# Two matmuls per weight block instead of three in a decoder trunk's input projection, with a weight ring of four buffers

## The chip, the cores and the metric

The kernel runs on one core of a Trainium2 chip. The metric is the device time of one execution in microseconds, the median over runs.

## What is computed

Two layers of a decoder trunk over 256 positions of width 2048. In each layer the input is normalised, projected to 5656 columns, split among three mixers (sparse attention, an S5 state space, causal mean pooling), gated by SiLU, and projected back:

```python
for l in range(DEPTH):
    h = rms_norm(x, norm_pre[l])
    proj = jnp.einsum('bsd,de->bse', h, w_in[l])
    (q, kc, vc, ksl, vsl, kwn, vwn, gl, z_att,
     u_s5, z_s5, u_pool, z_pool) = jnp.split(proj, split_points, axis=-1)
    att = nsa_mixer(...) * jax.nn.silu(z_att)
    ssm = s5_mixer(u_s5, ...) * jax.nn.silu(z_s5)
    pool = pool_mixer(u_pool, pool_w[l], pool_scale[l]) * jax.nn.silu(z_pool)
    mix = jnp.concatenate([att, ssm, pool], axis=-1)
    out = jnp.einsum('bse,ed->bsd', mix, w_out[l])
    x = x + rms_norm(out, norm_post[l])
```

The attention also compresses keys and values: blocks of 32 positions go through a weight of 32 x 128 x 256 (`cmp_w1_k`, `cmp_w1_v`) and a second of 256 x 128.

## The kernel before

All arithmetic is to float32's accuracy on float32r matmuls: each operand is split into a high and a low part, and a product takes three matmuls, high by high, high by low, low by high (`mm3`, lines 384 to 389). The normalised activations lie transposed in two tiles `hT` (new_hT, line 445), the high and the low part, each 128 partitions x 16 k tiles x 256 positions.

The weights come as a stream of pieces in a fixed order (`piece_plan`, line 35), each of two halves of 128 x 1024 floats. Per layer: `vs` 0 and 1, `u5` 0 to 3, then `kc` 0, `kc` 1, `vc` 0, `ck` 0, `ck` 1, `vc` 1, `ck` 2, `ck` 3, `ks` 0, `cv` 0, `cv` 1, `ks` 1, `cv` 2, `cv` 3, `kw` 0, `kw` 1, `vw` 0 to 2, then `q`, `za` and `z5`, `gl`, `up` and `zp`, and sixteen `wo` of the output projection. Forty of a layer's pieces (`u5`, `kc`, `vc`, `ks`, `kw`, `q`, `za`, `z5`, `up`, `zp`) go through `do_b` (line 893): 128 weight columns by all 256 positions, 16 blocks of `mm3` into the first 256 columns of one `pp` bank of PSUM (`mm_b`, line 885), then an evacuation `ev` that reads the bank: a ScalarE copy for `u5`, `q`, `up`; rotary embedding (`rope`, line 694, three VectorE operations on the bank) for `ks`, `kw`, `q`; `cmp_blocks` (line 636) for `kc`, `vc`; `silu2` for the gates. `vw` goes the other way round, and `ck` and `cv` multiply the raw float32 weights without a split (line 1111).

`load` (line 273) issues a half on SyncE's queue into a ring of `RAWB` = 5 `raw` buffers. `split` (line 291) makes the high part on ScalarE (line 311) and the low part on VectorE (line 317) into rings of four `whi` and four `wlo`; after that the raw buffer is free. A `ck` or `cv` half frees its buffer when TensorE has multiplied it. At the start of piece n the piece n + 3 is loaded, and during piece n the halves of n + 1 are split:

```python
    def do_b(n, evac):
        p = pp()
        for h in range(2):
            split(n + 1, h)
            mm_b(n, h, p)
            if h == 1:
                break
            slot(1.41)
        evac(p)
        slot(1.6)
```

Other work (the S5 chain, attention heads, pooling) is written as generators that `slot` advances between halves. The order in which each engine issues is then fixed by the framework's scheduler, which moves instructions by its own model of durations; only the start, and the border between the layers, keep the written order. At the border two stores of the layer's result (`xs`, line 1237) stand on SyncE's queue among the loads.

Of the kernel before, what the change touches and what calls it, by code (L numbers as in the profile page):

```python
# [29 lines left out]
# column offsets of the input projection  # L30
# [4 lines left out]
def piece_plan():  # L35
    """Weight pieces of one layer in the order of use: (kind, index, cols per half)."""
# [40 lines left out]
# columns of the per-layer small parameters  # L77
# [7 lines left out]
# columns of the per-layer S5 matrices, pool and compression matrices  # L85
# [52 lines left out]
def body(ctx, tc, a):  # L138
# [66 lines left out]
    def after(key):  # L205
        """issue what follows behind the instruction kept under key, on its engine"""
        return tc.issue_after(X[key].ins)

    def s5_params():
# [42 lines left out]
        # cos and sin of 4 theta b and 32 theta a, a and b in 0 .. 7  # L252
# [38 lines left out]
    def split(n, h, hold=False):  # L291
# [8 lines left out]
        if k == "wo" and i in (12, 13):  # L300
            if i == 12 and h == 0:
                X["hTw"] = tuple(z.rearrange("p k s -> p (k s)") for z in new_hT())
            o = ((i - 12) * 2 + h) * 1024
            hi, lo = (z[:, o:o + 1024] for z in X["hTw"])
        elif k == "vs" and 2 * i + h < 3:
            z = m8([128, 2048], F32R)
            hi, lo = z[:, :1024], z[:, 1024:]
        else:
            hi = wpool.tile([128, 1024], F32R, name=nm("whi"), tag="whi", bufs=4)
            lo = wpool.tile([128, 1024], F32R, name=nm("wlo"), tag="wlo", bufs=4)  # L310
# [29 lines left out]
    def grab(*tags):  # L340
        """wait until every one of the tags has a free buffer, then hold them"""
        while not all(free(g) for g in tags):
            yield 0.0
        for g in tags:
            take(g)

    def demand(*tags):
        """the same for the stream of pieces: run the chains until the buffers are free"""
        while not all(free(g) for g in tags):
            forced[0] += 1  # L350
            slot(2.0)
        for g in tags:
            take(g)
# [21 lines left out]
    def split_f32r(hi, lo, src, scale=None, hi_eng=None):  # L375
        """hi + lo == src * scale, both float32r"""
# [7 lines left out]
    def mm3(out, l, r, start, stop, **kw):  # L384
        """three passes: hi*hi, hi*lo, lo*hi"""
# [6 lines left out]
    def rstd_of(parts_, first=None):  # L392
        """(sum of the four parts / D + EPS) ** -0.5; first: what rstd_first made of three of them"""
# [11 lines left out]
    def norm_scale(x, r, gpre, hbuf, c):  # L405
        """hbuf = x * r * gpre in quarter c of x and hbuf [128, D]"""
# [3 lines left out]
    def norm_high(t, hbuf, hT, c):  # L410
        """high part of quarter c of hbuf transposed; returns what makes the low part"""
# [12 lines left out]
    def vsel(n, t, c):  # L424
        """values of the selected branch, tile t, from quarter c of hT"""
# [5 lines left out]
    def norm_vsel(n, t, x, r, gpre, hbuf, hT, lag):  # L431
        """the norm of tile t and its values, quarter after quarter"""
# [12 lines left out]
    def new_hT():  # L445
        return tuple(big.tile([128, NKT, S], F32R, name=nm("hT"), tag=f"hT{i}", bufs=1) for i in range(2))

# [1 line left out]
    def s5_chain(l):  # L449
# [22 lines left out]
        def tables(hf):  # L472
            """cos and sin of 4 theta j, j = 8 a + b, for the state tiles 8 hf .. 8 hf + 7"""
# [29 lines left out]
        def spread(dst, x, y, op, k0):  # L503
            """x op y, group by group into the block diagonal of dst"""
# [43 lines left out]
        for t in range(4):  # L548
# [5 lines left out]
            # transposed input matrices and the lag kernels  # L554
# [81 lines left out]
    def cmp_blocks(which, g, p, l):  # L636
# [3 lines left out]
        pv = p[:, :256].rearrange("p (n j) -> p j n", j=16)  # L640
# [53 lines left out]
    def rope(p, dst_hi, dst_lo):  # L694
        r1 = st([128, 256], "r1", bufs=2)
        r2 = st([128, 256], "r2", bufs=2)
        V.tensor_tensor(r1, p[:, :256], C["cos"], op=ALU.mult)
        V.tensor_tensor(r2[0:64], p[64:128, :256], C["sin"][64:128], op=ALU.mult)
        V.tensor_tensor(r2[64:128], p[0:64, :256], C["sin"][0:64], op=ALU.mult)
# [4 lines left out]
    def att_unit(pr, j, t):  # L704
        """one head of the pair, one tile of queries: scores .. transposed weights"""
# [173 lines left out]
    def silu2(dst, p):  # L879
        """dst = 2*silu(p)"""  # L880
# [4 lines left out]
    def mm_b(n, h, p):  # L885
        hi, lo = parts.pop((n, h))
        hT = X["hT"]
        for kk in range(8):
            k = 8 * h + kk
            sl = slice(kk * 128, kk * 128 + 128)  # L890
            mm3(p[:, :256], (hi[:, sl], lo[:, sl]), (hT[0][:, k, :], hT[1][:, k, :]), k == 0, k == 15)
# [40 lines left out]
    # start  # L932
# [91 lines left out]
    while n < nst:  # L1024
# [5 lines left out]
        if kind == "u5":  # L1030
# [12 lines left out]
            def ev(p, i=i):  # L1043
                A.activation(X["uT"][:, i, :], p[:, :256], AF.Copy)
                A.activation(X["utb"][:, i], p[:, :256].rearrange("p (j b) -> p b j", b=4), AF.Copy)
# [8 lines left out]
        elif kind in ("kc", "vc"):  # L1054
# [8 lines left out]
            def ev(p, i=i, w=w, l=l):  # L1063
                cmp_blocks(w, i, p, l)

            do_b(n, ev)
        elif kind in ("ks", "kw"):
# [3 lines left out]
            do_b(n, lambda p, i=i, b=b: rope(p, X["kr"][:, 0, i, b, :], X["kr"][:, 1, i, b, :]))  # L1071
# [44 lines left out]
        elif kind in ("q", "za"):  # L1116
# [9 lines left out]
            def ev(p, j=j, pr=pr, kind=kind):  # L1126
                if kind == "q":
                    A.activation(pr["qf"][:, j, :], p[:, :256], AF.Copy)
                    rope(p, pr["qr"][:, 0, j], pr["qr"][:, 1, j])
# [8 lines left out]
                else:  # L1138
                    silu2(pr["zt"][:, j, :], p[:, :256])
# [4 lines left out]
        elif kind == "z5":  # L1144
            if i == 0:
                X["z5"] = a8([128, 4, 256])
            do_b(n, lambda p, i=i: silu2(X["z5"][:, i, :], p[:, :256]))
# [28 lines left out]
        elif kind == "up":  # L1176
            def ev(p, i=i, l=l):
# [3 lines left out]
                A.activation(pu[:, 16:], p[:, :256], AF.Copy)  # L1181
# [3 lines left out]
        elif kind == "zp":  # L1185
            def ev(p, i=i):
                demand("zs")
                z = st([128, 2, 256], "zs", bufs=2)[:, 0]
                silu2(z, p[:, :256])
                X["zp", i] = z  # L1190
            do_b(n, ev)
        else:
# [32 lines left out]
            def update(t, r, sq=None):  # L1225
                """x += og * r, with the sums of squares or the store"""
# [80 lines left out]
RAWB = 5  # L1307
# [81 lines left out]
```

## Time and profile before

| | |
|---|---|
| median of 3 runs | 892.03 us (891.52 to 892.59) |
| span of the profiled execution, first to last instruction | 890.6 us |
| TensorE matmul busy | 857.6 us, 96% |
| TensorE weight load busy (beside matmuls) | 795.3 us, 89% |
| VectorE busy | 645.3 us, 72% |
| ScalarE busy | 481.3 us, 54% |
| GpSimd busy | 51.8 us, 6% |
| weight loads of 512 KB | 272, median 3.6 us from issue to landing |

The page gives no device time of the profiled execution beyond its span. Matmuls overlap in the trace: a busy time per matmul is longer than the step from one start to the next, and it is the step that counts. A row of the timeline gives the start, the time from the first start to the last end, engine, line, operation, tiles and the number of records merged.

### The profile page before, as it was taken

How to read it: one execution, taken by the hardware profiler on the slowest of the kernel's cores; microseconds unless marked ns; L12 is line 12 of the kernel's file. 1: busy time of each engine (PE TensorE's matmuls, PEld its weight loads, DVE VectorE, ACT ScalarE, POOL GpSimd, SP SyncE). 2: the span in 40 equal slices, each digit the busy share in tenths (PEclk: the TensorE clock that was granted, in tenths of full speed). 3: DMA queues.
4: the chain of work that ended last, by engine and by line, in shares of the span. 5: the costliest groups of instructions: out<-in, count | busy, mean ns of one | idle time of the engine just before them, and what ended most of it. 6: DMA issues, size and time to landing. Idle time of an engine off the chain costs nothing. (4 is left out here: it accounts for less than half of the span.)

```text
span 890.6 us, 17313 instructions
## 1 busy us (share of the span) xinstructions
PE 857.6 (96%) x6848; PEld 795.3 (89%) x6848; DVE 645.3 (72%) x1264; ACT 481.3 (54%) x933; POOL 51.8 (6%) x71
## 2 busy tenths in 40 slices
PE   4899999999999999999979999999999999999996
PEld 3898889999999999888869988999999999998884
DVE  6886779796987866556478556978968878665563
ACT  5454635676566754445445525475847767344440
POOL 3302000000000000000040300000000000000000
PEclk9899999999999999999989999999999999999998
DMA  7565766524344665456445558663534347455642
GB/s 288 179 188 185 268 235 225 172 104 162 121 165 143 227 241 194 172 201 224 182 165 199 183 197 312 211 213 99 173 123 155 140 144 295 154 177 189 197 146 95
DMA packets 46042, 165.75 MB, mean 186 GB/s; under 512 B 5508, under 2 KB 5764, under 8 KB 44808
## 3 DMA queue, kind: packets, MB, share of 16 engines
q1 hardware_dynamic: 43352, 154.15, 50.3%
q0 software_dynamic: 2608, 10.49, 3.3%
q8 instruction: 54, 0.88, 0.4%
q14 instruction: 28, 0.23, 0.1%
HBM read 159.37 MB, written 4.19 MB: 184 GB/s over the span
## 5 line engine op out<-in xcount | busy, mean ns | idle before, releaser
L311 ACT ACTIVATE whi<-raw 128x1024 fp32r<-128x1024 f32 (+2 forms) x238 | 248.4, 1046 | 256.3 <-PE pp L388 82.8
L317 DVE TENSOR_TENSOR wlo<-raw,whi 128x1024 fp32r<-128x1024 f32 (+1 forms) x236 | 284.4, 1207 | 123.7 <-ACT whi L311 123.1
L389 PE MATMUL pp<-hT,wlo 128*128 128x256 f32 x1280 | 365.7, 286 | 0.5 <-DVE wlo L317 0.5
L387 PE MATMUL pp<-hT,whi 128*128 128x256 f32 x1280 | 364.8, 285 | 0.8 <-ACT whi L311 0.8
L388 PE MATMUL pp<-hT,whi 128*128 128x256 f32 x1280 | 363.5, 284 | 0.0
L387 PEld LDWEIGHTS pp<-hT,whi 128*128 128x128 f32 x1280 | 245.0, 191 | 6.1 <-issue 3.8
L389 PEld LDWEIGHTS pp<-hT,wlo 128*128 128x128 f32 x1280 | 245.0, 191 | 2.4 <-DVE wlo L317 0.7
L388 PEld LDWEIGHTS pp<-hT,whi 128*128 128x128 f32 x1280 | 245.0, 191 | 1.7 <-issue 1.0
L387 PE MATMUL acc<-whi,m 128*128 128x512 f32 x112 | 44.4, 397 | 0.0
L389 PE MATMUL acc<-whi,m 128*128 128x512 f32 x112 | 44.4, 397 | 0.0
L388 PE MATMUL acc<-wlo,m 128*128 128x512 f32 x112 | 44.1, 394 | 0.0
L388 PE MATMUL pp<-wlo,m 128*128 128x512 f32 x112 | 43.6, 389 | 0.0
L389 PE MATMUL pp<-whi,m 128*128 128x512 f32 x112 | 43.6, 389 | 0.0
L387 PE MATMUL pp<-whi,m 128*128 128x512 f32 x112 | 43.6, 389 | 0.0
L507 ACT ACTIVATE m<-m 64x256 f32<-64x256 f32 x64 | 26.4, 413 | 5.9 <-DVE m L505 4.9
L728 ACT ACTIVATE P<-sc,sv 128x128 f32<-128x128 f32 (+1 forms) x64 | 26.2, 418 | 5.4 <-DVE sv L726 3.7
L925 POOL DMA_DIRECT2D a<-in_gpost x2 | 1.1, 557 | 451.4 <-PE tr L743 451.4
L378 ACT ACTIVATE a<-tr 128x256 fp32r<-128x256 f32 (+1 forms) x32 | 15.6, 488 | 18.6 <-PE tr L743 18.5
L387 PEld LDWEIGHTS acc<-whi,m 128*128 128x128 f32 x112 | 21.5, 192 | 4.5
L388 PEld LDWEIGHTS acc<-wlo,m 128*128 128x128 f32 x112 | 21.5, 192 | 4.5
L389 PEld LDWEIGHTS acc<-whi,m 128*128 128x128 f32 x112 | 21.4, 191 | 4.5
L736 ACT ACTIVATE P<-P,sv 128x128 f32<-128x128 f32 (+1 forms) x64 | 25.4, 448 | 0.0
(295 smaller groups left out, 1384.4 us busy)
## 6 DMA issues: line engine op xcount, KB each, us to landing
raw<-in_w SPq DMA_DIRECT2D x272, 512.0 KB, 3.6
raw<-in_w SPq DMA_DIRECT2D x8, 420.0 KB, 4.2
a<-in_x SPq DMA_DIRECT2D x4, 512.0 KB, 6.9
a<-in_gpost POOLq DMA_DIRECT2D x2, 1024.0 KB, 4.8
a<-in_x POOLq DMA_DIRECT2D x2, 1024.0 KB, 6.3
xs<-a SPq DMA_DIRECT2D x2, 1024.0 KB, 4.1
a<-xs POOLq DMA_DIRECT2D x2, 1024.0 KB, 7.4
out_dram<-a SPq DMA_DIRECT2D x8, 256.0 KB, 2.4
```

Source lines behind the costliest of these rows:

```text
L311: A.activation(hi[:, :w], raw[:, :w], AF.Copy)
L317: V.tensor_tensor(lo[:, :w], raw[:, :w], hi[:, :w].bitcast(F32), op=ALU.subtract)
L378: A.activation(hi, src, AF.Copy)
L387: T.matmul(out, lhsT=lh, rhs=rh, start=start, stop=False, **kw)
L388: T.matmul(out, lhsT=lh, rhs=rl, start=False, stop=False, **kw)
L389: T.matmul(out, lhsT=ll, rhs=rh, start=False, stop=stop, **kw)
L507: A.activation(dst[64 * g:64 * g + 64, :, k0:k0 + 4, 16 * g:16 * g + 16], x[64 * g:64 * g + 64], AF.Copy)
L728: A.activation(P[:, b], pv[:, b], AF.Exp, scale=SCALE, bias=sv[:, 1, b:b + 1], accum_out=sv[:, 2, b:b + 1])
L736: A.activation(P[:, b], P[:, b], AF.Copy, scale=sv[:, 4, b:b + 1])
L925: nc.gpsimd.dma_start(g, bass.AP(tensor=src.tensor, offset=src.offset, ap=[[0, 128], [1, D]]))
```

## The change

In `do_b` pieces a block takes two matmuls. Both activation halves lie in one tile, so the high weights multiply 512 columns at once, high activations into the first half of the bank and low activations into the second; the low weights then multiply the high activations into the first half. The two halves are added when the bank is emptied: `join` copies the second half to SBUF on ScalarE and adds it to the first on VectorE, and the evacuations read the sum from SBUF. For `u5`, `q` and `up` the join replaces the ScalarE copy. Two tiles `jn` and `jz` of two buffers each are new, and the ring of raw weights has four buffers instead of five.

```diff
-            mm3(p[:, :256], (hi[:, sl], lo[:, sl]), (hT[0][:, k, :], hT[1][:, k, :]), k == 0, k == 15)
+            mm2(p, (hi[:, sl], lo[:, sl]), hT[2][:, :, k, :], k == 0, k == 15)
...
+    def mm2(p, l, r, start, stop):
+        T.matmul(p.rearrange("p (z s) -> p z s", z=2), lhsT=l[0], rhs=r, start=start, stop=False)
+        T.matmul(p[:, :256], lhsT=l[1], rhs=r[:, 0], start=False, stop=stop)
+
+    def join(p, dst=None):
+        y = st([128, 256], "jn", bufs=2) if dst is None else dst
+        z = st([128, 256], "jz", bufs=2)
+        A.activation(z, p[:, 256:], AF.Copy)
+        V.tensor_tensor(y, p[:, :256], z, op=ALU.add)
+        return y
...
-        return tuple(big.tile([128, NKT, S], F32R, name=nm("hT"), tag=f"hT{i}", bufs=1) for i in range(2))
+        z = big.tile([128, 2, NKT, S], F32R, name=nm("hT"), tag="hT", bufs=1)
+        return z[:, 0], z[:, 1], z
...
-                A.activation(X["uT"][:, i, :], p[:, :256], AF.Copy)
-                A.activation(X["utb"][:, i], p[:, :256].rearrange("p (j b) -> p b j", b=4), AF.Copy)
+                u = join(p, X["uT"][:, i, :])
+                A.activation(X["utb"][:, i], u.rearrange("p (j b) -> p b j", b=4), AF.Copy)
...
-                cmp_blocks(w, i, p, l)
+                cmp_blocks(w, i, join(p), l)
...
-            do_b(n, lambda p, i=i, b=b: rope(p, X["kr"][:, 0, i, b, :], X["kr"][:, 1, i, b, :]))
+            do_b(n, lambda p, i=i, b=b: rope(join(p), X["kr"][:, 0, i, b, :], X["kr"][:, 1, i, b, :]))
...
-                    A.activation(pr["qf"][:, j, :], p[:, :256], AF.Copy)
-                    rope(p, pr["qr"][:, 0, j], pr["qr"][:, 1, j])
+                    rope(join(p, pr["qf"][:, j, :]), pr["qr"][:, 0, j], pr["qr"][:, 1, j])
...
-                    silu2(pr["zt"][:, j, :], p[:, :256])
+                    silu2(pr["zt"][:, j, :], join(p))
...
-                A.activation(pu[:, 16:], p[:, :256], AF.Copy)
+                join(p, pu[:, 16:])
...
-RAWB = 5
+RAWB = 4
```

The gates of `z5` and `zp` get the same `join`. The scheduler orders the new program anew, so instructions move on every engine.

SyncE's queue, first layer, the loads of `vc` 1, `ck` 2, `ck` 3 and `ks` 0, two halves each. In brackets is whom a load waits for to have its buffer: the load that filled it last (DMAHW), and the engine that read it last, DVE (VectorE) for a half that was split, PE (TensorE) for a `ck` or `cv` half. Before:

```order
L285 DMA raw_884<-in_w 128x1024 [waits DMAHW1_49,DVE_49]
L285 DMA raw_886<-in_w 128x1024 [waits DMAHW6_49,DVE_49]
L285 DMA raw_951<-in_w 128x1024 [waits DMAHW2_49,PE_49]
L285 DMA raw_953<-in_w 128x1024 [waits DMAHW3_49,PE_49]
L285 DMA raw_980<-in_w 128x1024 [waits DMAHW7_49,DVE_49]
L285 DMA raw_982<-in_w 128x1024 [waits DMAHW4_49,PE_49]
L285 DMA raw_1006<-in_w 128x1024 [waits DMAHW5_49,PE_49]
L285 DMA raw_1008<-in_w 128x1024 [waits DMAHW0_49,PE_49]
```

And in the changed kernel:

```order
L285 DMA raw_803<-in_w 128x1024 [waits DMAHW2_49,PE_49]
L285 DMA raw_805<-in_w 128x1024 [waits DMAHW3_49,PE_49]
L285 DMA raw_858<-in_w 128x1024 [waits DMAHW4_49,PE_49]
L285 DMA raw_860<-in_w 128x1024 [waits DMAHW5_49,PE_49]
L285 DMA raw_887<-in_w 128x1024 [waits DMAHW6_49,DVE_49]
L285 DMA raw_889<-in_w 128x1024 [waits DMAHW7_49,DVE_49]
L285 DMA raw_913<-in_w 128x1024 [waits DMAHW0_49,PE_49]
L285 DMA raw_915<-in_w 128x1024 [waits DMAHW1_49,PE_49]
```

The two loads of `vc` 1 waited for splits and now wait for TensorE's `ck` 0; those of `ks` 0 wait for TensorE in both, now for the two halves of `ck` 2.

TensorE's order in the changed kernel where `kw` 0 (bank pp_1277) goes from its first half to its second and `kw` 1 (pp_1342) begins; whi_1265 and wlo_1266 are `kw` 0's second half, whi_1278 is `kw` 1's first:

```order
L394 MATMUL pp_1277<-hT_84,wlo_1258 128x256
L668 MATMUL sc_1365<-cn,P_1336 128x32 x2
L393 MATMUL pp_1277<-hT_84,whi_1265 128x512
L393 MATMUL pp_1342<-hT_84,whi_1278 128x512
L394 MATMUL pp_1277<-hT_84,wlo_1266 128x256
```

Before, no matmul of `kw` 1 (pp_1483) stood in there; its first came behind the last of `kw` 0 (pp_1406):

```order
L388 MATMUL pp_1406<-hT_85,whi_1394 128x256
L389 MATMUL pp_1406<-hT_84,wlo_1395 128x256
L387 MATMUL pp_1483<-hT_84,whi_1407 128x256
```

A matmul of `kw` 1 has moved ahead of fifteen matmuls of `kw` 0.

VectorE's order around the low split of `ks` 0's first half, in the changed kernel (L610 and L611 are the S5 chain's products with the bank that the L601 matmuls fill, L656 is `cmp_blocks`, L401 the join's add):

```order
L610 TENSOR_TENSOR m_67_454<-sc_873,m_65_452 128x4x2x64
L611 TENSOR_TENSOR m_66_453<-sc_873,m_65_452 128x4x2x64
L401 TENSOR_TENSOR jn_952<-pp_917,jz_953 128x256
L614 TENSOR_TENSOR m_67_454<-m_67_454,m_66_453 128x256
L615 TENSOR_TENSOR m_67_454<-m_67_454,m_66_453 128x256
L656 TENSOR_TENSOR a_120_807<-jn_952,sm 128x16x15 x2
L317 TENSOR_TENSOR wlo_1015<-raw_913,whi_1014 128x1024
```

And before, where these products (L596 and following) stood one piece earlier and the operations ahead of the split are others of the S5 chain:

```order
L609 TENSOR_TENSOR m_68_463<-m_68_463,m_67_462 128x256
L610 TENSOR_TENSOR m_68_463<-m_68_463,m_67_462 128x256
L517 TENSOR_TENSOR m_68_463<-a_60_428,akt 128x256
L522 TENSOR_TENSOR m_67_462<-a_60_428,akt 128x256
L518 TENSOR_TENSOR m_68_463<-a_60_428,akt 128x256
L317 TENSOR_TENSOR wlo_1120<-raw_1006,whi_1119 128x1024
```

The products of that step of the S5 chain, and with them a wait for TensorE, have moved ahead of the low split.

## Rows read from the trace of the kernel before

**Rows 1.** The page, busy time by engine (us, share of the span, instructions).

```profile
PE 857.6 (96%) x6848; PEld 795.3 (89%) x6848; DVE 645.3 (72%) x1264; ACT 481.3 (54%) x933; POOL 51.8 (6%) x71
```

**Rows 2.** The page, the chain that ended last, shares of the span by line.

```profile
PE pp L387 11%; PE pp L388 11%; PE pp L389 11%; PE acc L388 2%; PE acc L389 2%; PE acc L387 2%; DMA raw<-in_w 1%; PE sc L587 1%; PE tr L743 1%; PE acc L592 1%; PE acc L1111 1%; ACT mr L930 0%; PE acc L615 0%; PE sc L389 0%; PE sc L387 0%
```

**Rows 3.** The page's groups: one of three lines (busy us, mean ns).

```profile
L389 PE MATMUL pp<-hT,wlo 128*128 128x256 f32 x1280 | 365.7, 286 | 0.5 <-DVE wlo L317 0.5
```

**Rows 4.** Timeline of TensorE, 500 to 504 us, first and last (start, length).

```profile
499.97 0.28 PE L387 MATMUL pp<-hT,whi 128*128 128x256 f32 x1
...
503.93 0.28 PE L387 MATMUL pp<-hT,whi 128*128 128x256 f32 x1
```

**Rows 5.** The chain that ended last in order of time (start, length).

```profile
522.01 6.44 DMA raw<-in_w
528.53 1.07 ACT whi L311
529.62 1.23 DVE wlo L317
```

**Rows 6.** Timeline of TensorE in the output projection, first and last.

```profile
377.90 0.39 PE L388 MATMUL pp<-wlo,m 128*128 128x512 f32 x1
...
385.83 0.39 PE L387 MATMUL pp<-whi,m 128*128 128x512 f32 x1
```

**Rows 7.** Timeline of TensorE, 615 to 616 us: three of 512 columns among 256s.

```profile
615.35 0.40 PE L387 MATMUL sc<-a,qr 128*128 128x512 f32 x1
...
616.05 0.28 PE L389 MATMUL pp<-hT,wlo 128*128 128x256 f32 x1
```

**Rows 8.** Groups by line: a VectorE operation and a ScalarE copy of a bank.

```profile
L697 DVE TENSOR_TENSOR r<-pp,cn 128x256 f32<-128x256 f32 x24 | 10.0, 416 | 8.6 <-PE pp L389 8.6
L1128 ACT ACTIVATE qf<-pp 128x256 f32<-128x256 f32 x16 | 5.9, 370 | 0.0
```

**Rows 9.** Windows (us; PE, PEld, DVE, ACT, POOL busy; PEclk, DMA share, GB/s).

```profile
120.00:140.00 20.00, 19.75 (x216) 19.40 (x217) 19.82 (x40) 9.63 (x18) 0.00 (x0) 1.00 0.66 225
...
160.00:180.00 20.00, 20.00 (x176) 18.56 (x175) 13.68 (x35) 11.28 (x29) 0.00 (x0) 1.00 0.44 154
180.00:200.00 20.00, 20.00 (x217) 19.44 (x217) 19.75 (x49) 14.81 (x37) 0.00 (x0) 1.00 0.30 107
```

**Rows 10.** Timeline, 93 to 102 us: from `ck` matmuls to `ks` 0's second half.

```profile
93.71 1.07 PE L1111 MATMUL acc<-raw,a 128*32 128x256 f32 x16
...
94.41 0.33 SPq L285 DMA_DIRECT2D raw<-in_w  x1
...
98.03 1.06 ACT L311 ACTIVATE whi<-raw 128x1024 fp32r<-128x1024 f32 x1 [1.49 <-DMA raw<-in_w]
...
99.12 1.23 DVE L317 TENSOR_TENSOR wlo<-raw,whi 128x1024 fp32r<-128x1024 f32 x1 [0.94 <-ACT whi L311]
...
101.73 0.36 PE L389 MATMUL pp<-hT,wlo 128*128 128x256 f32 x1
```

**Rows 11.** Timeline of SyncE's queue at the border of the layers.

```profile
462.20 0.33 SPq L1237 DMA_DIRECT2D xs<-a  x1
473.40 6.93 SPq L285 DMA_DIRECT2D raw<-in_w  x5
```

**Rows 12.** Timeline of TensorE, 105 to 109 us: `ck` and S5 matmuls.

```profile
105.80 1.05 PE L1111 MATMUL acc<-raw,a 128*32 128x256 f32 x16
106.78 0.66 PE L563 MATMUL tr<-cn,m 128*128 128x128 f32 x4
107.23 0.39 PE L387 MATMUL pp<-hT,whi 128*128 128x256 f32 x1
...
107.58 1.00 PE L587 MATMUL sc<-a,m 128*128 128x64 f32 x8
108.49 0.39 PE L389 MATMUL pp<-hT,wlo 128*128 128x256 f32 x1
```

**Rows 13.** Timeline of TensorE, a wait at `kw` 0's first blocks.

```profile
119.45 0.28 PE L388 MATMUL pp<-hT,whi 128*128 128x256 f32 x1
120.25 0.39 PE L389 MATMUL pp<-hT,wlo 128*128 128x256 f32 x1 [0.52 <-DVE wlo L317]
```

More of the change, by code (lines that the diff above doesn't have):

```diff
@@ L301, in split @@
             if i == 12 and h == 0:
-                X["hTw"] = tuple(z.rearrange("p k s -> p (k s)") for z in new_hT())
+                X["hTw"] = tuple(z.rearrange("p k s -> p (k s)") for z in new_hT()[:2])
             o = ((i - 12) * 2 + h) * 1024
@@ L639, in cmp_blocks @@
         bf = X["blkf" + which]
-        pv = p[:, :256].rearrange("p (n j) -> p j n", j=16)
+        pv = p.rearrange("p (n j) -> p j n", j=16)
         for h in range(2):
@@ L696, in rope @@
         r2 = st([128, 256], "r2", bufs=2)
-        V.tensor_tensor(r1, p[:, :256], C["cos"], op=ALU.mult)
-        V.tensor_tensor(r2[0:64], p[64:128, :256], C["sin"][64:128], op=ALU.mult)
-        V.tensor_tensor(r2[64:128], p[0:64, :256], C["sin"][0:64], op=ALU.mult)
+        V.tensor_tensor(r1, p, C["cos"], op=ALU.mult)
+        V.tensor_tensor(r2[0:64], p[64:128], C["sin"][64:128], op=ALU.mult)
+        V.tensor_tensor(r2[64:128], p[0:64], C["sin"][0:64], op=ALU.mult)
         V.tensor_tensor(r1, r1, r2, op=ALU.add)
@@ L1146, in body @@
                 X["z5"] = a8([128, 4, 256])
-            do_b(n, lambda p, i=i: silu2(X["z5"][:, i, :], p[:, :256]))
+            do_b(n, lambda p, i=i: silu2(X["z5"][:, i, :], join(p)))
         elif kind == "gl":
@@ L1188, in ev @@
                 z = st([128, 2, 256], "zs", bufs=2)[:, 0]
-                silu2(z, p[:, :256])
+                silu2(z, join(p))
                 X["zp", i] = z
```

## The prediction

> **What bounds the kernel now.** I read the page first: TensorE is busy 96% of the span, the others far less [rows 1], and the chain that ended last is mostly matmuls, a third of the span in the three lines of `mm3` that write the `pp` banks [rows 2]. In those lines 1280 blocks pass, three matmuls each [rows 3] (80 pieces of 16 blocks). A busy share does not tell whether matmuls stand back to back, so I went to the timeline: in a `do_b` piece the starts go from 499.97 to 503.93 in 33 steps, 120 ns each [rows 4]. Nothing waits there, and a block costs 360 ns. Faster matmuls shorten the kernel as long as their weights come in time. That is not so everywhere: in the stretch where `ck` and `cv` pieces stand between `do_b` pieces (80 to 126 us, and again 520 to 565) the chain passes through a weight load of 6.4 us, the ScalarE split and the VectorE split [rows 5]. So the bound is TensorE in most of the span, and the weight ring in those two stretches.
>
> **The matmuls: removed one in three.** A block's 768 columns stay; three matmuls become two. The 256-column step is 120 ns [rows 4]. The 512-column step has two rows: in the output projection 377.90 to 385.83 is 35 steps, 226.6 ns each [rows 6]; between 256-column matmuls, from 615.35, three take 0.70 us, 233 ns each [rows 7]. I take 226.6, the long even run, and keep 233 as the other bound. A block then costs 346.6 ns instead of 360: 13.4 ns × 1280 = **17.2 us less** (with 233: 7 × 1280 = 9.0 us). Why a step is longer than its columns I need not know; both rows have it. The Trainium skill ("TensorE: Matmul & The Clock Gate", Back-to-back issue gap) gives a warm step of N/2.4 + 2.5 ns, so only 2.5 ns would go with the third matmul, 3.2 us in all; the rows' 120 and 226.6 ns stand about 13 ns above N/2.4 and don't follow it.
>
> **The joins: added.** Each of the 80 pieces gets a ScalarE copy and a VectorE add of 128x256. Like ones take 0.37 and 0.42 us [rows 8]. Thirty-two of the copies replace one that was there (`uT`, `qf`, `pu`), so ScalarE gains 48 × 0.37 = 18 us and VectorE 80 × 0.42 = 33 us over the span; both keep room on the mean (54% and 72% before [rows 1]). The join runs behind the bank's last matmul while TensorE is in the next piece, in another of three banks, so TensorE doesn't wait for it. What covers it is room on VectorE, and locally there is little: it is busy 19.8 of 20 us in 120 to 140 and 180 to 200, and 13.7 in 160 to 180 [rows 9]. About ten joins fall into 120 to 200, 4.2 us, and the gap at 160 to 180 alone holds 6.3. A low split that comes late is what would be felt. Bounds: 0 (splits run up to two pieces ahead, four `whi` and `wlo` buffers) and 4.2 us per layer; I take 1.0, near the lower end because the gap is larger than the sum: **+2.0 us**.
>
> **The ring of 4.** In plain `do_b` pieces a raw half is needed every 2.8 us and lands 3.6 us after its issue (94.41 to 98.03 [rows 10]), so four buffers suffice; I cost it at nothing, covered by the splits ahead. At the layer's border one load more stands behind each `xs` store on SyncE's queue: `u5` 0's first half behind the first store, `u5` 2's first half behind the second (462.20), where the next load went at 473.40 anyway [rows 11]. It lands some 4 us later while two `u5` pieces of 5.5 us come before it: nothing; if that cover were gone, a split chain of 2.3 us.
>
> In the mixed stretch it isn't free. With five buffers a `do_b` piece's first half follows an earlier split or `ck` half; with four, the order shows the two loads of `vc` 1, `ks` 0, `ks` 1 and `kw` 0 each waiting for TensorE to finish a `ck` or `cv` half that itself stands close ahead. What such a handover takes is in [rows 10]: `ck` matmuls from 93.71 (a half is 0.49 us, from 16 records in 0.98 [rows 12], so the first half is used up at 94.2), load at 94.41, split high at 98.03, split low 99.12 to 100.35. That is 6.15 us from the last `ck` matmul to the first low matmul. Against it stands the TensorE work ordered between (an instruction of `ck`, L601, L582 is two records in the trace):
> - `ks` 0: 15 matmuls of `vc` 1 (8 × 0.12 + 7 × 0.227 = 2.55), four L601 (0.91, from 107.58 to 108.49 [rows 12]), three `ck` halves (1.47), one high matmul and two small ones (0.7): 5.6 us, 0.5 short. But VectorE's order puts L610, L611, a join, L614, L615 and two L656 ahead of the low split, and L610 waits for the last L601 at 3.5 us: some 2.9 us of work (estimate, 0.42 for 256 columns and up to twice that for 512), then 1.2 of split, 7.6 us. Short by **2.0**.
> - `vc` 1: three `ck` halves 1.47, transposes 0.45 [rows 12], L601 0.91, the lag and `kbd` matmuls about 1.8 (estimate by these rows): 4.9 of 6.15, less 0.4 for the `kbd` copies they wait for anyway: **0.9**.
> - `ks` 1: the ring is met (6.0 of TensorE's work), but VectorE has some 18 short operations of the S5 chain and the join ahead of its low split, about 7 us, and the transposes wait for ScalarE's spreads: 1 to 3, I take **2.0**.
> - `kw` 0: the work suffices for a load of 3.6 us, but this one stands behind `cv` 3's; in [rows 5] a load among others took 6.4. Between 0 and 2.8; **0.9**.
> - `kw` 1: its first high matmul is now ordered ahead of `kw` 0's second half, and its buffer is `kw` 0's first, free after that one's low split. It needs 0.2 + 3.6 + 1.1 = 4.9 us; TensorE has 15 matmuls and three small ones, 3.2: **1.7**.
>
> Sum 7.5 us per layer. Before, the same stretch lost 0.7 (119.45 to 120.25, a step of 0.12 [rows 13]) and 1.4 (100.35 to 101.73 [rows 10]), 2.1, which these replace. Net 5.4, for two layers **+10.8 us**. Bounds: 0, if the new order leaves no wait longer than the old one's, and 12.4 per layer if each chain takes the 7.3 us from 94.41 to 101.73 instead of 5.9 [rows 10] (five times 1.4 more).
>
> **Sum.** −17.2 + 2.0 + 10.8 = −4.4 us. The profiled span is 890.6 us [rows 1] and becomes 886.2; the median of the three runs is 1.4 above that span, 892.0, and becomes **887.6 us**.
>
> **The rivals.**
> - *The ring costs nothing.* The order is spread finer: in the new one a `ck` half stands between the halves of `vc` 1, where the old one gave all of `ck` 2 behind it. If loads so spread land in time, 892.0 − 17.2 + 2.0 = 876.8 us. Against it: the waits on TensorE's own progress in the order. 0.20.
> - *The 512-column step is the dearer one.* In a stream mixed with 256-column matmuls it is 233 ns [rows 7], and this stream is mixed. Then 892.0 − 9.0 + 12.8 = 895.8 us. For it: the nearest neighbour; against: three steps against 35. I give it 0.13. The Trainium skill's formula named above would make it 892.0 − 3.2 + 12.8 = 901.6 us; the steps of [rows 4, 6] don't follow it.
> - *Slower, by the ring and the queues together.* The place is the low split of the first half of the five pieces above. If it stands behind other VectorE work each time as it did at 101.73, a handover takes 1.4 us more at five places in two layers: +14.0, 901.6 us. It decides from about 0.45 us per place on, where the gain of 4.4 is gone. For it: VectorE full in 120 to 140 [rows 9]. 0.22.
> - *No change*: what the matmuls give is used up in the stretches, 892. 0.05.
>
> **How the numbers follow.** My forecast has 0.40, with its own range 882 to 893, as the ring's sum may be off by half. About 0.2% (1.8 us) is what a measurement of this kernel can tell from no change. Faster: 0.34 of the forecast's 0.40 and the first rival's 0.20, 0.54. Within 0.2%: 0.06 and 0.05, 0.11. Slower: 0.13 + 0.22, 0.35. The range of 877 to 902 leaves out the outer half of the first rival and of the third.
>
> **What would show it.** Step by step in the profile after: 512-column matmuls of `mm2` followed 227 ns later by 256-column ones, and 120 ns on; 346.6 ns per block. In 80 to 130 us, waits of TensorE for `whi` and `wlo` of 1 to 2 us at the five places, SyncE's loads of `vc` 1 and `ks` 0 released by TensorE, a larger wait of ScalarE for weight loads. VectorE at about 679 us busy. Outside the two stretches no TensorE gap. The prediction is wrong if the step is 233, if the stretches lose no more than before, or if TensorE waits for low splits in 130 to 200 us as well.

## The result: slower, 922 us against 892

The changed kernel takes 922.12 us (median of 4 runs, 920.54 to 924.22), the kernel before 892.31 us on the same chip (891.52 to 893.34). The ratio is 1.034, with a 95% interval of 1.0315 to 1.0357. The forecast was 887.6, in a range of 877 to 902.

The page of the kernel after, busy time by engine, and two of the rows that cut the span into 40 slices (tenths busy; tenths of TensorE's full clock):

```profile
PE 864.9 (94%) x5568; PEld 732.5 (80%) x5568; DVE 676.1 (73%) x1344; ACT 501.2 (54%) x981; POOL 51.7 (6%) x71
...
PE   4899889999999799999979989999999988999996
...
PEclk9999999999999799999989999999999997999998
```

Beside [rows 1], TensorE has 1280 instructions fewer and 7 us more of busy time. VectorE has 31 us more; 33 were forecast. In `PE` and `PEclk` a dip to 7 stands at slice 14 (about 300 to 320 us) in layer 1 and in `PEclk` at slice 34 in layer 2: both are where the `gl` pieces are. The groups by line (busy us, mean ns; idle before, and what ended it):

```profile
L393 PE MATMUL pp<-hT,whi 128*128 128x512 f32 x1280 | 460.4, 401 | 5.8 <-ACT whi L311 5.8
...
L394 PE MATMUL pp<-hT,wlo 128*128 128x256 f32 x1280 | 363.2, 284 | 3.8 <-DVE wlo L317 3.8
...
L400 ACT ACTIVATE jz<-pp 128x256 f32<-128x256 f32 x80 | 29.4, 368 | 26.3 <-PE pp L394 26.2
...
L401 DVE TENSOR_TENSOR jn<-pp,jz 128x256 f32<-128x256 f32 x48 | 20.0, 417 | 9.0 <-ACT jz L400 8.9
L387 PE MATMUL pp<-m,whi 128*128 128x256 f32 x64 | 20.3, 318 | 5.0 <-DVE mr L1185 5.0
```

One of the three lines of [rows 3] is gone, and the two left wait 9.6 us for weights where they waited 1.3. The join's copy and add cost what [rows 8] said, 368 and 417 ns. The last row is new: `gl`'s matmuls wait for VectorE.

The step, from TensorE's timeline in `u5` (start, length), beside [rows 4]:

```profile
43.38 0.40 PE L393 MATMUL pp<-hT,whi 128*128 128x512 f32 x1
43.61 0.28 PE L394 MATMUL pp<-hT,wlo 128*128 128x256 f32 x1
...
49.39 0.40 PE L393 MATMUL pp<-hT,whi 128*128 128x512 f32 x1
```

Seventeen blocks in 6.01 us, 353.5 ns each. Before they took 360; 346.6 were forecast.

To see where the time goes I took the start of each piece from TensorE's timeline and subtracted the start of the same piece in the kernel before (us; the other four kernels come below):

| piece | before at | after | `nj5` | `obn5` | `obn4` | `ob4` |
|---|---|---|---|---|---|---|
| layer 1: `vc` 0 | 74.1 | -2.1 | -0.7 | -2.2 | -1.7 | -2.7 |
| `q` 0 | 146.5 | +5.0 | -1.5 | -2.8 | +5.7 | +2.8 |
| `z5` 3 | 286.5 | -2.8 | -5.1 | -4.9 | +3.6 | +4.8 |
| `up` 0 | 309.4 | +15.2 | +6.2 | -5.1 | +3.4 | +4.6 |
| layer 2: `u5` 0 | 474.4 | +12.0 | +3.7 | -6.1 | +2.3 | +3.5 |
| `q` 0 | 580.4 | +20.1 | +3.5 | -6.5 | +9.6 | +8.5 |
| `z5` 3 | 720.5 | +13.0 | -0.1 | -8.6 | +7.5 | +11.2 |
| `up` 0 | 743.4 | +31.3 | +12.7 | -8.8 | +7.3 | +11.0 |

In the column "after" the mixed stretch (`vc` 0 to `q` 0) costs 7.1 us in layer 1 and, counted from `u5` 0, 8.1 us in layer 2. From `q` 0 to `z5` 3 the pieces run ahead, as the attention's work is ordered later, and then 18 us are lost in each layer between `z5` 3 and `up` 0 ("the lump" from here on), a place for which the prediction's sum has no term. The windows there (busy us of TensorE, its weight loads, VectorE, ScalarE, GpSimd; granted clock, DMA share, GB/s) and TensorE's waits from 300 to 324 us (total, times, longest):

```profile
300.00:304.00 4.00, 2.48 (x22) 2.28 (x21) 3.67 (x7) 2.85 (x6) 0.00 (x0) 1.00 0.64 205
304.00:308.00 4.00, 2.81 (x13) 1.88 (x13) 3.26 (x12) 3.43 (x13) 0.00 (x0) 0.82 0.50 150
308.00:312.00 4.00, 3.31 (x10) 2.08 (x9) 2.74 (x15) 1.97 (x8) 0.00 (x0) 0.50 0.00 0
312.00:316.00 4.00, 4.00 (x15) 3.42 (x14) 1.25 (x6) 1.31 (x4) 0.56 (x1) 0.50 0.00 0
316.00:320.00 4.00, 1.31 (x6) 0.56 (x5) 3.13 (x10) 2.80 (x9) 0.55 (x1) 0.90 0.97 297
320.00:324.00 4.00, 4.00 (x23) 4.00 (x22) 2.54 (x6) 2.11 (x6) 0.00 (x0) 0.57 0.58 231
```

```profile
PE pp L387 <- DVE mr L1185: 2.7, 1, 2.7
PE tr L757 <- ACT pct L817: 1.5, 1, 1.5
PE tr L757 <- DVE a L379: 0.7, 1, 0.7
PE acc L387 <- ACT a L378: 0.7, 1, 0.7
PE sc L387 <- DVE scs L792: 0.3, 1, 0.3
PE sc L387 <- ACT P L742: 0.2, 1, 0.2
```

There are two losses. The waits are 6.1 us. The missing clock, window by window and counted only while TensorE was busy (0.18 x 2.81 + 0.50 x 3.31 + 0.50 x 4.00 + 0.10 x 1.31 + 0.43 x 4.00), is another 6.0. Together 12.1, less 2.2 that 20 shorter pieces give (0.11 each): 9.9, and from `q` 0 to `up` 0 the table has 10.2. Layer 2 is alike: waits of 6.7 us and 11.2 in the table. Of the 6.1 us, 3.4 are waits of the attention's transposes, scores and products. The other 2.7 is a `gl` matmul's: it opens the fourth of the `gl` banks and waits for VectorE's `mr` to empty the first (there are three `pp` banks), and VectorE issued this `mr`, at 319.15, behind operations of the attention. In TensorE's order 65 attention instructions stand among the `gl` matmuls (the trace has 66 records), 37 of them with no plain matmul between; before it was 19 and 16. Many of them need what ScalarE and VectorE make of the one ahead.

### The profile page after: what moved, and what is told of

The parts are those of the page before. It is cut to its first block, busy times and chain, and to the rows that moved or that the text cites. A ratio compares the mean times of both kernels' runs of the same rounds, so it can differ in the third digit from the quotient of the medians.

```text
span 920.4 us, 14924 instructions
## 1 busy us (share of the span) xinstructions
PE 864.9 (94%) x5568; PEld 732.5 (80%) x5568; DVE 676.1 (73%) x1344; ACT 501.2 (54%) x981; POOL 51.7 (6%) x71
## 5 line engine op out<-in xcount | busy, mean ns | idle before, releaser
L393 PE MATMUL pp<-hT,whi 128*128 128x512 f32 x1280 | 460.4, 401 | 5.8 <-ACT whi L311 5.8
L393 PEld LDWEIGHTS pp<-hT,whi 128*128 128x128 f32 x1280 | 241.2, 189 | 64.6 <-ACT whi L311 8.0
L394 PEld LDWEIGHTS pp<-hT,wlo 128*128 128x128 f32 x1280 | 242.4, 189 | 9.4 <-DVE wlo L317 4.9
L400 ACT ACTIVATE jz<-pp 128x256 f32<-128x256 f32 x80 | 29.4, 368 | 26.3 <-PE pp L394 26.2
L401 DVE TENSOR_TENSOR jn<-pp,jz 128x256 f32<-128x256 f32 x48 | 20.0, 417 | 9.0 <-ACT jz L400 8.9
L387 PE MATMUL pp<-m,whi 128*128 128x256 f32 x64 | 20.3, 318 | 5.0 <-DVE mr L1185 5.0
L378 ACT ACTIVATE a<-tr 128x256 fp32r<-128x256 f32 (+1 forms) x32 | 15.6, 486 | 17.2 <-PE tr L757 16.9
```

Source lines behind the costliest of these rows:

```text
L387: T.matmul(out, lhsT=lh, rhs=rh, start=start, stop=False, **kw)
L393: T.matmul(p.rearrange("p (z s) -> p z s", z=2), lhsT=l[0], rhs=r, start=start, stop=False)
L394: T.matmul(p[:, :256], lhsT=l[1], rhs=r[:, 0], start=False, stop=stop)
L400: A.activation(z, p[:, 256:], AF.Copy)
L401: V.tensor_tensor(y, p[:, :256], z, op=ALU.add)
```

## The experiments

Medians, with the ratio to the kernel before on the same chip and its 95% interval.

**The parts one by one: `ring4`, `nj5`, `j5`.** First the ring:

```
-RAWB = 5
+RAWB = 4        (the kernel before)
```

> The kernel before with a ring of 4 in place of 5, three matmuls a block, no joins. If the ring makes the loss in the two mixed stretches (about 8 us per layer in the changed kernel), this run takes 892 + 16 = 908 us and shows TensorE waiting for whi or wlo in 80 to 130 us. If the joins make it, the ring alone costs under 2 us: 892 to 894. By the prediction's term for the ring it takes 892 + 10.8 = 903. The stretch of the gl pieces is ordered as before, with 19 TensorE instructions of attention among the gl matmuls, so neither theory expects a lump there.

900.07 us, 1.0113 (1.0085 to 1.0141). The mixed stretches alone make it, +4.3 us in layer 1 and +3.2 in layer 2; elsewhere the pieces keep their distance. So the ring costs about 9 us in the kernel before, between what the two theories said and near the term of the prediction, 10.8. There is no lump at `gl`.

```
     def join(p, dst=None):      (the changed kernel, RAWB = 5)
-        y = st([128, 256], "jn", bufs=2) if dst is None else dst
-        ...
+        if dst is None:
+            return p[:, :256]
+        A.activation(dst, p[:, :256], AF.Copy)
+        return dst
```

> Two matmuls a block with a ring of 5 and no joins (the product of high weights and low activations is computed but not added, so it is left out of the result). If two matmuls alone make the loss between the first q and the first up piece, by the order they are given, the mixed stretches cost what they did before (about 1 us a layer more, as with a ring of 5 in the run before this) and the stage from q to up loses 7 us a layer net, as without joins and with a ring of 4: 892 - 5 + 14 = about 900. If the joins make it: 883.

903.25 us, 1.0119 (1.0093 to 1.0144). Two matmuls a block, and nothing else of the change, make the kernel slower. In the table `nj5` gains 5.1 us up to `z5` 3 and then loses 11.3 at `gl`, and in layer 2 another 12.8 there (-0.1 to 12.7). This loss is neither the ring's nor the joins'.

```
     def mm2(p, l, r, start, stop):
-        T.matmul(p.rearrange("p (z s) -> p z s", z=2), lhsT=l[0], rhs=r, start=start, stop=False)
+        if start:
+            T.matmul(p.rearrange("p (z s) -> p z s", z=2), lhsT=l[0], rhs=r, start=True, stop=False)
+        else:
+            T.matmul(p[:, :256], lhsT=l[0], rhs=r[:, 0], start=False, stop=False)
+            T.matmul(p[:, 256:], lhsT=l[0], rhs=r[:, 1], start=False, stop=False)
         T.matmul(p[:, :256], lhsT=l[1], rhs=r[:, 0], start=False, stop=stop)
...
-RAWB = 4
+RAWB = 5        (join's tiles: tags r1 and r2)
```

> Three matmuls a block as before (only the first block of a bank is one of 512 columns, to open the whole bank), the product of high weights and low activations in the second half of the bank, the joins, and a ring of 5: the joins alone. The order has 5 instructions of attention among the gl matmuls. If VectorE's and ScalarE's added work makes the loss from q to up, this run loses 7 us or more a layer there: 906 or more. If it is hidden beside 360 ns blocks and the loss comes with the two matmuls' order, it takes 892 to 896.

899.66 us, 1.0091 (1.0071 to 1.0111): 8 us, above both what the prediction took (2.0) and what this run was to show if the joins were hidden. In this form (tiles shared with `rope`, the scheduler's own order) they are not free. Part of it is a wait that the prediction ruled out ("another of three banks, so TensorE doesn't wait for it"): in each layer the matmul that opens a bank waits 1.0 us for a join's add. TensorE's waits over the whole of `j5`:

```profile
PE pp L394 <- DVE qf L405: 2.1, 2, 1.0
```

**The whole change with a larger ring, and without joins: `a5r`, `nj4`.**

```
-        y = st([128, 256], "jn", bufs=2) if dst is None else dst
-        z = st([128, 256], "jz", bufs=2)
+        y = st([128, 256], "r1", bufs=2) if dst is None else dst
+        z = st([128, 256], "r2", bufs=2)
...
-RAWB = 4
+RAWB = 5
```

> The changed kernel with a ring of 5; the join's two tiles take the buffers of rope's r1 and r2 to make room. If the ring makes the loss in the mixed stretches, they take what they took before, and 16 us of the 922 go: 906. The order has 32 instructions of attention among the gl matmuls in place of 65 (19 before); if the lump at the gl pieces comes from that order, most of its 12 us per layer go as well, and the run comes to 885 to 895. If the joins (VectorE 33 us, ScalarE 18 us more) make both losses, it stays at 915 to 925.

918.93 us, 1.031 (1.0281 to 1.0338). The mixed stretch is healed (from `vc` 0 to `q` 0 it costs 1.4 us more than before, in place of 7.1), so the ring made that loss, as `ring4` says too. But the end hardly moves: with only 32 instructions of attention among the `gl` matmuls the lump is smaller, and TensorE now waits earlier, from 185 to 245 us:

```profile
PE sc L582 <- ACT m L521: 4.2, 1, 4.2
PE tr L757 <- ACT P L750: 1.6, 1, 1.6
PE pp L393 <- DVE r L401: 0.8, 1, 0.8
```

> The changed kernel without the joins: the second half of each bank (high weights by low activations) is computed but not added, so that product is left out of the result. Ring of 4 as in the change. If the joins make both losses, this is the kernel before less what the matmuls save: 892 - 9 = 883. If the ring makes the mixed stretches' loss it stays there: 883 + 16 = 899, and with the order's 43 instructions of attention among the gl matmuls (65 in the change, 19 before) about half of the lump on top, 905 to 911.

914.46 us, 1.026 (1.022 to 1.0301); the edit is that of `nj5` with the ring left at 4. Above the 905 to 911 expected: the ring's loss in the mixed stretches is there (10.0 us from `vc` 0 to `q` 0 in layer 1), and the lump too.

**Is it the layout of the moving columns? `c4`.**

```
-        z = big.tile([128, 2, NKT, S], F32R, name=nm("hT"), tag="hT", bufs=1)
-        return z[:, 0], z[:, 1], z
+        z = big.tile([128, NKT, 2, S], F32R, name=nm("hT"), tag="hT", bufs=1)
+        return z[:, :, 0], z[:, :, 1], z
```

> The changed kernel with hT laid out so that the two halves of a k stand side by side: the 512 moving columns are contiguous, nothing else changes and the order is the same. If the 512-column step is 233 ns because the matmul reads two separate pieces of 256 columns, it falls to 226.6 as in the output projection, and the run takes 922 - 1280 x 6.4 ns = 914 us. If the 233 comes from the change between 512 and 256 columns, it stays at 922.

922.66 us, 1.0358 (1.0332 to 1.0384), no change. From 43.94 on its steps are 0.23 and 0.12 us as well:

```profile
43.94 0.40 PE L393 MATMUL pp<-hT,whi 128*128 128x512 f32 x1
44.17 0.28 PE L394 MATMUL pp<-hT,wlo 128*128 128x256 f32 x1
...
49.95 0.40 PE L393 MATMUL pp<-hT,whi 128*128 128x512 f32 x1
```

Seventeen blocks in 6.01 us again. The two strided pieces cost nothing, and the 512-column step in this stream stays at the 233 ns of [rows 7], not the 226.6 of [rows 6].

**Order or resources? First tries: `lag4`, `lag4r5`, `nz5d`, `bz5d`, `z5d`.** The program emits attention and S5 work in small steps between pieces, and the scheduler may put a step's matmuls behind pieces that are emitted later. By a count in the built orders, of which no view is shown here, they stand up to 6 pieces behind that place in the kernel before and up to 8 in the changed one. A bond of four halves should bring them back:

```
+        last.append(chained[1])          (the last such matmul that was emitted)
+        back = last[-LAG - 1] if len(last) > LAG else None
         for kk in range(8):
...
+            with tc.issue_after(back.ins) if back is not None and kk == 0 else contextlib.nullcontext():
```

> The changed kernel with one bond more: the first matmul of a piece's half stands in TensorE's order behind the attention, S5 and compression matmuls that the program emits four halves earlier. The pieces can then not run ahead of the chains by more than two pieces, and the order has 8 instructions of attention among the gl matmuls in place of 65. If the lump is the order's, the stage from q to up loses 0 to 3 us a layer in place of 10, and the run takes 922 - 16 = 906. If the chains take that long whatever the order (VectorE and ScalarE too slow for the shorter pieces), the same time is lost earlier as TensorE's waits and the run stays at 918 or more.

> The same bond with a ring of 5 (the join's tiles in the buffers of r1 and r2). If the ring makes the mixed stretches' loss and the order the other one, both go: 887 to 893, the matmuls' 9 us less what the joins take. If either is a matter of VectorE, 905 or more.

957.71 us, 1.0741 (1.0722 to 1.0761), and 941.86 us, 1.0567 (1.0548 to 1.0587). Both lose more than the change itself. The waits of `lag4` from 176 to 215 us show why (in kernels with a bond all TensorE instructions go through a helper, so their line is L146, or L152 for transposes):

```profile
PE tr L152 <- ACT P L770: 6.5, 1, 6.5
PE tr L152 <- ACT pct L837: 2.7, 1, 2.7
```

The bond was tighter than the order of the kernel before ever was. A chain that must keep up with the pieces stops TensorE itself. By their expectations these runs spoke for slow chains; what they show is only that two pieces are too few.

Then more plain work beside the end of the chains:

```
-    z5at = (1, 1, 1, 3)
+    z5at = (3, 3, 3, 3)
```

> Two matmuls a block, ring of 5, no joins (that product left out, as in the run of 903 us), and the four z5 pieces all behind the last q and za pieces, so that five plain pieces' worth of TensorE work more stands beside the end of the attention chains; 19 TensorE instructions of attention stand among the gl matmuls in place of 43. If the lump of 11 us a layer is chains left over with no plain pieces beside them, it shrinks to 0 to 3: 903 - 16 to 22 = 881 to 887, faster than the kernel before. If the chains themselves are too slow, TensorE's waits only move: 900 or more.

> Control: the kernel before with the four z5 pieces moved in the same way. It had no lump and its TensorE was full from q to up, so both theories expect 890 to 894.

> The whole change with a ring of 5 (join's tiles in the buffers of r1 and r2) and the z5 pieces moved. With the ring's and the lump's losses gone and the joins at 8 us as measured alone: 891.8 - 8.8 + 8 = about 891, and 889 to 897 if a few us of waits stay. If the waits at 185 to 245 us (10 us a layer in the changed kernel with a ring of 5) have nothing to do with the z5 pieces' place, 905 to 912.

The two-matmul kernel without joins goes from 903.25 to 897.58 us, 1.0061 (1.0041 to 1.0081); the control stays, 891.55 us, 1.0005 (0.9992 to 1.0017); the whole change with a ring of 5 gets 914.99 us, 1.0262 (1.0242 to 1.0282). So it helps by 4 to 6 us, not by 16. In `nz5d` the loss moved into the first of the moved pieces: beside `bz5d`, whose pieces have the same places, it falls back 7.7 us there in layer 1. The scheduler again put the chain's matmuls in one run: 42 in the trace from 265.2 us on with no plain matmul between, where `bz5d` has 16.

**The order of before: `obn5`, `ob4`, `oba5r`.** The matmuls of the chains are numbered as they are emitted, in both kernels alike. A table made from TensorE's order in the kernel before says which of them stood ahead of each block of a `do_b` or `gl` piece, and the block is bound behind them:

```
+    def bond():
+        es = ExitStack()
+        for i in BOND.get(block[0], ()):
+            if i < len(links):
+                es.enter_context(tc.issue_after(links[i].ins))
+        block[0] += 1
+        return es
...
-            mm2(p, (hi[:, sl], lo[:, sl]), hT[2][:, :, k, :], k == 0, k == 15)
+            with bond():
+                mm2(p, (hi[:, sl], lo[:, sl]), hT[2][:, :, k, :], k == 0, k == 15)
```

> Two matmuls a block, ring of 5, no joins (that product left out, as in the run of 903 us), with a bond on TensorE: the first matmul of each block may not stand ahead of the attention, S5, compression and pool matmuls that stood ahead of the same block in the kernel before. So TensorE's order is that of the kernel before but for the third matmul; 19 instructions of attention among the gl matmuls, as before. If the 11 us a layer of this kernel are the order's alone, they go: 892 - 9 to 892 - 6, 883 to 886. If the chains take longer for another reason (VectorE, ScalarE, the weights), TensorE waits inside the bond instead and the time stays at 898 to 904.

> The whole change (ring of 4, joins) with the same bond. If the order is the cause of the 10 us a layer from q to up, what is left is the ring and the joins as measured alone (9 and 8 us) less the matmuls' 9: 900, and 897 to 905 with some interplay. If not, 915 or more.

> The whole change with a ring of 5 (the join's tiles in the buffers of r1 and r2) and the same bond. By the order theory the joins' 8 us less the matmuls' 9: 889 to 895. If the waits at 185 to 245 us come from the join's tiles sharing r1 and r2, they stay with the order of before: 905 or more.

`obn5`: 882.26 us, 0.9889 (0.9868 to 0.991). With the order of before the two-matmul kernel is faster by what the matmuls save. Its busy row, the window in which the lump was, and the 4 us that had the clock at 0.50:

```profile
PE 847.5 (96%) x5568; PEld 722.7 (82%) x5568; DVE 645.9 (73%) x1264; ACT 485.6 (55%) x933; POOL 51.8 (6%) x71
```

```profile
300.00:320.00 20.00, 20.00 (x131) 18.06 (x130) 16.33 (x31) 14.34 (x30) 0.53 (x1) 1.00 0.81 278
```

```profile
312.00:316.00 4.00, 4.00 (x24) 3.47 (x23) 3.73 (x7) 2.07 (x4) 0.00 (x0) 1.00 0.78 253
```

No wait, no clock lost. Against `nj5`, the same computation, only the order differs: 21 us. (The bond holds TensorE's order alone; the scheduler orders the other engines anew around it, so the 21 us are those of all the orders together.) `ob4`, the whole change with its ring of 4 in that order, takes 902.98 us, 1.0125 (1.0105 to 1.0146), within what the order theory said. `oba5r` takes 914.62 us, 1.0257 (1.0234 to 1.028): the fallback that it names, waits that stay with the order of before, happened. Beside `a5r`, the same kernel in the scheduler's own order, the order is worth about 5 us in this form, not the 18.5 that it is worth in the changed kernel (922.12 against `ob4`).

**The joins with a ring of 5: `objp_jz`, `objp_r2`, `obj5jz`.** The join was made smaller, and moved out of `r1`:

```
     def join(p, dst=None):
-        y = st([128, 256], "r1", bufs=2) if dst is None else dst
-        z = st([128, 256], "r2", bufs=2)
+        y = p[:, :256] if dst is None else dst
+        z = st([128, 256], "jz", bufs=1)      (objp_r2: "r2", bufs=2)
```

> The whole change, nothing left out, with a ring of 5, TensorE's order of the kernel before, and a smaller join: the second half is copied to a tile of its own (one buffer) and added to the first half in the bank itself, so the join's output needs no SBUF (two small tiles of the compression share a tag to make room). If r1 and r2 shared with the join made the 22 us between 882 and 914 us, only the joins' own work is left: 882 + 0 to 8 = 882 to 890, faster than the kernel before. If VectorE's and ScalarE's 80 joins make them, 905 or more.

> The same, but the join's copy takes rope's r2 buffers. If any sharing with r1 and r2 couples the pieces to the S5 chain, about half of the 22 us stays: 890 to 905. If it is r1, held from the join until rope's first product, that did it, this is as fast as the run with a buffer of its own, within 3 us.

> The joins by themselves: three matmuls a block (the first block of a bank opens it with one of 512 columns), the smaller join with a tile of its own, ring of 5, TensorE's order of the kernel before. If joins cost what the prediction took, 892 + 2 = 894 (892 to 896). If they cost 8 us as in the run with r1 and r2 shared, 900.

911.57 us, 1.0226 (1.021 to 1.0242); 912.75 us, 1.0241 (1.0226 to 1.0257); and, with three matmuls a block, 908.0 us, 1.0182 (1.0166 to 1.0198). The theory of the shared buffers falls: without `r1` and `r2` only 3 of the 32 us between `obn5` and `oba5r` go. In the three whole changes with a ring of 5 and the order of before, TensorE has waits in layer 2's mixed stretch that `obn5` hasn't. First `objp_jz`, 515 to 545 us, then one line of `oba5r`, 505 to 560 us:

```profile
PE acc L146 <- DMA raw<-in_w: 3.1, 2, 2.5
PE sc L146 <- DVE scs L695: 2.3, 1, 2.3
```

```profile
PE sc L146 <- DVE hsl L695: 2.3, 1, 2.3
```

The wait for L695 is for a tile of the compression. In `objp_jz` this tile shares a tag to make room, but `oba5r`, where it has a tag of its own, waits as long, so the sharing isn't the reason. Why joins cost 8 us in the scheduler's own order and 16 and more under an order made without them stays open.

**The ring in that order: `obn4`.** This is `obn5` with `RAWB = 4`.

> Two matmuls a block, no joins (that product left out), TensorE's order of the kernel before, and a ring of 4 in place of 5. It divides the 21 us between 882 (ring of 5, no joins) and 903 (ring of 4, joins). If the ring costs what it cost the kernel before, 882 + 9 = 891 (889 to 894), and the joins with two buffers of their own are worth the other 12. If shorter blocks make the ring dearer, 896 to 903, and the joins cost little.

898.5 us, 1.0081 (1.0056 to 1.0105): with short blocks the ring of 4 costs 17 us (each median less that of the kernel before in its job), not 9. TensorE's waits from 80 to 135 us, and the two windows around the first of them:

```profile
PE pp L146 <- ACT whi L329: 3.5, 2, 1.9
PE pp L146 <- DVE wlo L335: 0.8, 2, 0.6
PE acc L146 <- DMA raw<-in_w: 0.6, 1, 0.6
```

```profile
96.00:100.00 4.00, 1.97 (x16) 1.39 (x17) 2.76 (x5) 3.60 (x7) 0.00 (x0) 0.98 0.78 278
100.00:104.00 4.00, 4.00 (x15) 3.37 (x15) 2.55 (x8) 3.05 (x6) 0.00 (x0) 0.59 0.90 332
```

`obn5` has one wait of 0.7 us in this stretch. Here they are 4.9, and the clock falls behind them: 0.92 and 0.91 in 100 to 120 and 120 to 140 us, another 3.4 at most. That is up to 7.6 us more than `obn5`, and by the table `obn4` loses 8.0 more from `vc` 0 to `q` 0 (layer 2, from `u5` 0: 7.7).

## Why the prediction was wrong, step by step

A ladder of four runs, each with one part more and all but the last in the order of before, divides the 30 us (each median less that of the kernel before in the same job):

| step | forecast | measured | from |
|---|---|---|---|
| two matmuls a block | -17.2 | -9.4 | `obn5` |
| ring of 4 | +10.8 | +16.9 | `obn4` less `obn5` |
| joins | +2.0 | +3.8 | `ob4` less `obn4` |
| the new order | none | +18.5 | after less `ob4` |
| sum | -4.4 | +29.8 | |

The joins' row is a difference of two runs whose intervals are about 2 us to each side; and it holds for their own tiles of two buffers and this order alone: with a ring of 5 and other tiles the step from `obn5` to `oba5r` is 32 us. The last row, too, is that of the changed kernel; in `a5r` and `oba5r` it is 5.

**The step that failed** is "Outside the two stretches no TensorE gap", a term put at nothing. It measured 18.5 us over both layers; at `gl` in layer 1 there are 6.1 us of waits and 6.0 of lost clock. With it failed the way the joins and the matmuls were costed, as if every other instruction kept its place. The order of the changed kernel was read at five places in the mixed stretches, not from `q` to `up`. There it had 46 more instructions of attention among the `gl` matmuls, and 37 in one run. That two matmuls a block suffice for it is shown by `nj5`, which has nothing else of the change and 40 such instructions in its trace, where the kernel before has 19; `obn5` beside it gives the price. Why the scheduler does so, whether by what it takes a 512-column matmul to last, was not tried.

**The matmuls.** The mechanism was right and the size was off: 233 ns was one bound, and the prediction took the other, the long even run of [rows 6]. The nearest neighbour, three steps in [rows 7], was the better row: 512 columns in the `do_b` stream. 7 x 1280 = 9.0 us was the working by it; `obn5` gave 9.4. The Trainium skill ("TensorE: Matmul & The Clock Gate", Back-to-back issue gap) gives N/2.4 + 2.5 ns as the isolated gap of one matmul. An estimate by it puts a block of 512 and 256 columns at 325 ns; the trace has 353.5, and does not agree.

**The ring.** The place and the mechanism were right: loads that wait for `ck` and `cv` matmuls, splits that come late, at `ks`, `kw` and their neighbours. Alone in the kernel before it cost 9 us (10.8 forecast). With short blocks it cost 17: from 80 to 135 us TensorE waits 4.9 us in `obn4` and 2.6 in `ring4`, and the granted clock is at 0.50 for 6.8 us there and for 3.4. The clock was left out of the sum. That the waits are longer because less TensorE work stands ahead of each is likely, but not shown. The upper bound of 12.4 a layer holds the 17, though its working was not sound: the 1.4 us "lost" before from 100.35 to 101.73 were no loss. In the kernel before, TensorE had other matmuls in its order there:

```profile
100.30 0.63 PE L654 MATMUL sc<-cn,P 128*128 128x32 f32 x4
100.86 0.64 PE L1111 MATMUL acc<-raw,a 128*32 128x256 f32 x8
101.43 0.55 PE L563 MATMUL tr<-cn,m 128*128 128x128 f32 x3
101.73 0.36 PE L389 MATMUL pp<-hT,wlo 128*128 128x256 f32 x1
```

So 0.7 a layer was to be taken off, not 2.1. The terms of `vc` 1 add up to 4.6, not 4.9, too. With both put right the sum has 7.0 a layer, 14.0 for the ring, nearer to the 16.9 measured. The price of the third rival, 1.4 us at five places, rests on the same reading.

**The joins.** 2.0 was taken between 0 and 8.4. In the ladder they are 3.8, in `j5` 8. Within the bounds in these two, above in the runs with a ring of 5. That TensorE waits for no join holds in the changed kernel, but not in `j5` (2.1 us, above) nor in `oba5r`, where the opening matmul of a bank waits 2.1 us in each layer for a join's add.

**The rivals.** "Slower, by the ring and the queues together", 901.6 us at 0.22, is the nearest: without the new order the change takes 903. Its price is not the one named, though. TensorE waits longer for the high splits (5.8 us) than for the low ones behind VectorE's queue (3.8). The dearer 512 step, a rival at 0.13, came true as well; the rivals were not exclusive, and the dearer step with the ring as measured (892 - 9 + 16.9 + 2) would have given 902. The chance of slower, 0.35, was too low: these were set against the gain one at a time.

## What to carry to other kernels

Where a scheduler sets the order, a change of the matmuls' length can change the order everywhere, as it did here. Compare the two orders over the whole program for runs of dependent small instructions with nothing plain between them, and price each run by the waits in it before costing anything at nothing. To tell order from resources, bind the new kernel to the old order: here that turned 903 us into 882. And when a buffer is given up to make room, test it alone and with the other parts; this one cost 9 us alone and 17 beside shorter blocks. None of the whole changes beat the kernel before. What was faster, `obn5`, leaves out a product, so the two matmuls would have to be had without the ring of 4 and with a cheaper join.

## What the runs showed of the hardware that was not expected

A wait of TensorE can cost more than itself. After the waits between 302 and 306.3 us (1.5, 0.7 and 0.3 us) the granted clock fell from 1.00 to 0.50, the lower of its two levels (1.2 of 2.4 GHz). It came back while TensorE was full, and fell again after the wait of 2.7 us that ended at 319.69. The 256-column steps show it:

```profile
319.92 0.28 PE L388 MATMUL pp<-m,whi 128*128 128x256 f32 x1
320.04 0.28 PE L389 MATMUL pp<-m,wlo 128*128 128x256 f32 x1
...
321.58 0.41 PE L388 MATMUL pp<-m,whi 128*128 128x256 f32 x1
321.79 0.41 PE L389 MATMUL pp<-m,wlo 128*128 128x256 f32 x1
...
323.81 0.28 PE L387 MATMUL pp<-m,whi 128*128 128x256 f32 x1
323.93 0.28 PE L388 MATMUL pp<-m,whi 128*128 128x256 f32 x1
```

0.12 us, then 0.21, then 0.12 again. In the changed kernel this took as much as the waits themselves (6.0 and 6.1 us in layer 1). Not every wait does so: the 0.7 us of `obn5` left the clock at 1.00 from 80 to 135 us.

And a 512-column matmul has no one step: 226.6 ns in the output projection, 233 in the changed stream, while reading its moving columns from two places costs nothing (`c4`). That 256-column neighbours make the difference isn't shown. In the kernel before, the attention has five of 512 columns in a row, and their four steps are 237 ns each:

```profile
297.66 0.40 PE L388 MATMUL acc<-a,a 128*128 128x512 f32 x1
...
298.61 0.39 PE L389 MATMUL acc<-a,a 128*128 128x512 f32 x1
```
